# Output projections in 512 columns, weights in units of 1 MB, norm rows kept for the last block, the sample group moved to the third

## The chip, the cores and the metric

The kernel runs on one core of a Trainium2 chip, in one launch. The metric is the time of the launch in device microseconds. The engines are named as in the profile: PE is TensorE (matmuls and transposes), PEld its loads of the stationary operand, DVE is VectorE, ACT is ScalarE, POOL is GpSimd and SP is SyncE, which here only issues transfers (DMAs) in the order of its queue.

## What is computed

One inference step of a decoder trunk of two layers, for a prompt group of 2048 rows and a sample group of 8 rows (one token each, with 2048 cached rows per sequence), which share the weights. The model width is 1024. Cut to what matters here:

```python
for layer in range(2):
    # layer 0: spatial-gating MLP (A) beside stick-breaking attention (B)
    # layer 1: top-256 sparse attention with an indexer (C) beside causal pooling (D)
    hp = mixer(xp @ w_in[layer])          # (2048, 1024)
    hs = mixer(xs @ w_in[layer], cache)   # (8, 1024)
    xp = layer_norm(alpha * xp + hp @ w_out[layer], ln_g[layer], ln_b[layer])
    xs = layer_norm(alpha * xs + hs @ w_out[layer], ln_g[layer], ln_b[layer])
```

All values are float32. The caches' new rows are outputs too.

## The kernel before

**Tiling.** The prompt is cut into four blocks of 512 rows (`TB`). For each block and layer there is an input projection (`p0` for layer 0, `p1a` and `p1b` for layer 1), the mixers (`mixer_b`, and `c_tiles` over 16 query tiles of 128 rows), and an output projection with the norm (`out_proj`, `ln_late`, `ln`). Each projection splits both operands into a high and a low part in the format fp32r and sums three products, high x high, low x high and high x low: L876 to L878 for the input, L1261 to L1263 for the output. The input projection holds 128 columns of weights stationary (`wh`, `wl`) and moves 512 rows of x; the output projection holds 128x128 of the mixers' output (`oh`, `ol`) stationary and moves 256 columns of the weights, into one PSUM tile `pp_o` for each 128 rows. DVE adds `pp_o` to the rows `xres` (L1266).

**Weights.** `plan_w` lists pieces of 512 KB in the order of use, `more_w` loads the next one when a piece has been used, and `load_w` fetches it: raw into `wr`, then ACT copies out the high part (L749) and DVE subtracts to get the low part (L752). Weights of layer 1 are split at the first block and kept in DRAM in two parts; later blocks load both parts (L744). `wh` and `wl` have two buffers each; every third kept piece goes into the two buffers of `wr` instead (`THIRD`).

**Sample group.** Its rows pass through each projection beside one prompt block: `ps_smp` (L894) in the input projection, `ps_so` (L1274) in the output projection. In layer 1 its attention (`sample1`) gathers the cached values through a table of pages with 16 indirect DMAs that POOL issues (L2425, tile `s_vp`, two buffers), and PE uses each gather in L2429 (`ps_sv`). Its last output projection and its norm stand beside the fourth block: `xs_res` are its residual rows, `xpre` its rows before the norm in DRAM, `xs_ln` the rows that are normed.

**Norm.** `ln` computes statistics on DVE (L1325, L1326, a reciprocal root of 15 small operations, then `ln_nb`), scales on ACT (L1339), multiplies with g on POOL (L1340) and adds b on DVE (L1341). The rows of g and b (`lng`, `lnb`) are loaded for each call and half of the columns, 256 KB each (L1335, L1336). The last 128 rows of the last block are projected apart in `out_tail` (L1292 to L1296), when the last attention tile is done; the weights for that lie in a pool `tw`, opened when the pools of the selection (`sel`) close.

**Order of the work.** `run` interleaves streams by estimated costs (`par`), which decides only in which order the program is recorded. Afterwards a planner (`Order`) simulates the engines with its own table of costs and writes a fixed order for each engine and the turn in which tiles get their buffers. Any change of sizes or buffers therefore gives a new order on all five engines. Each engine runs its order strictly in sequence.

Of the kernel before, what the change touches and what calls it, by code (L numbers as in the profile page):

```python
# [11 lines left out]
F32 = mybir.dt.float32  # L12
# [27 lines left out]
THIRD = True  # L40
# [4 lines left out]
KT = 8  # L45
# [654 lines left out]
class Body:  # L700
# [31 lines left out]
    def load_w(self, src, shape, key, pool=None):  # L732
        nc = self.nc
        wr = lambda d, n: self.loc.tile(shape, d, tag="wr", name=n, bufs=self.bufs["wr"])
        new = lambda d, n: (pool or self.wp).tile(shape, d, tag=n, name=n, bufs=4 if pool else 2)
        if shape[2] == 64:
            return self.load_idx(src, key)
# [8 lines left out]
        raw = wr(F32, "wr")  # L746
        nc.sync.dma_start(raw, src)
        hi, lo = new(F32R, "wh"), new(F32R, "wl")
        nc.scalar.copy(hi, raw)  # L749
        h = shape[1] // 2  # L750
        for e, c in ((nc.vector, slice(0, h)), (nc.vector, slice(h, 2 * h))):
            e.tensor_tensor(lo[:, c], raw[:, c], hi[:, c].bitcast(F32), op=OP.subtract)  # L752
        if KEEP.get(key[0]) == key[1]:
            kept = self.kept_w[key[::2]] = [self.dr.tile(shape, F32, name="w%s_%s_%s" % (n, key[0], "_".join(map(str, key[2])) if isinstance(key[2], tuple) else key[2])) for n in "hl"]
            for t, d in zip((hi, lo), kept):
                nc.sync.dma_start(d, t.bitcast(F32))
        return hi, lo

    def load_idx(self, src, key):

        nc = self.nc
        w = self.wp.tile([P, KT, P], F32R, tag="wh", name="wi2")
        kept = self.kept_w.get(key[::2])
        if kept:
            nc.sync.dma_start(w.bitcast(F32), kept)
        else:
            raw = self.loc.tile([P, KT, 64], F32, tag="wr", name="wr", bufs=self.bufs["wr"])
            nc.sync.dma_start(raw, src)
            nc.scalar.copy(w[:, :, 0:64], raw)
            nc.vector.tensor_tensor(w[:, :, 64:P], raw, w[:, :, 0:64].bitcast(F32), op=OP.subtract)  # L770
            kept = self.kept_w[key[::2]] = self.dr.tile([P, KT, P], F32, name="wi2d")
            nc.sync.dma_start(kept, w.bitcast(F32))
        return w[:, :, 0:36], w[:, :, 64:100], w
# [42 lines left out]
    def load_x(self, src):  # L816
# [3 lines left out]
        for kt in range(KT):  # L820
            x = self.otile("xc")
            nc.sync.dma_start(x, src[kt * P:(kt + 1) * P])
# [37 lines left out]
    def proj(self, m, x, smp, c0):  # L860
# [22 lines left out]
        self.more_w()  # L883
# [73 lines left out]
    def plan_w(self, stages):  # L957

        I = self.I
        self.wplan, self.wready, self.kept_w, self.n_kept = [], [], {}, 0  # L960
        for no, st in enumerate(stages):
            key = st, stages[:no].count(st)
            if st[:3] == "out":
                w = I["w_out"][int(st[3])]
                self.wplan += [(w[cg, hf], [P, 4, 256], (*key, (cg, hf)))
                               for cg in range(4) for hf in HALVES[int(st[3])]]
                continue
# [5 lines left out]
            self.wplan += [(w(c, n), [P, KT, 64 if n == 36 else n], (*key, c)) for c, n in cols]  # L973
        for _ in range(2):
            self.more_w()

    def more_w(self, pool=None):
        if self.wplan:
            src, shape, key = self.wplan.pop(0)
            self.wready.append(self.load_w(src, shape, key, pool))  # L980
# [1670 lines left out]
```

## Time and profile before

| what | before |
|---|---|
| median of 3 runs | 2663.24 us (2654.11 to 2670.14) |
| the profiled execution | 2654.22 us |
| its span, first to last instruction | 2652.5 us |
| PE busy | 2552.0 us |
| DVE, ACT, POOL busy | 1951.7, 1483.4, 747.4 us |
| mean granted clock of PE | 0.986 |
| bytes by DMA | 582.34 MB, 220 GB/s over the span |

Busy times are unions over the time axis: matmuls are pipelined, so the sum of their durations is more than PE's busy time, and the distance between two starts says how long one occupies PE. A wait is idle time of an engine, put down to what ended it. "Landing" is when a transfer's data has arrived. The profiled execution is 9.0 us faster than the median of the runs.

### The profile page before, as it was taken

Reading aid. Unit: us, or ns where it says so; the run is one execution under the profiler, and the core shown is the slowest. Engines: PE = TensorE matmul, PEld = TensorE weight load, DVE = VectorE, ACT = ScalarE, POOL = GpSimd, SP = SyncE. Lnnn points to the kernel's source line nnn. Section 1 sums busy time; section 2 is a strip of 40 time slices with the busy share of each in tenths; the row PEclk is TensorE's granted clock in tenths of the full one; section 3 lists DMA queues with packets and bytes.
Section 4 is the critical chain, followed back from the end, with each engine's and each line's share of the span. In section 5 each row is a group of like instructions: output and inputs, shape, how many; then the busy total and the mean of one; then the engine's idle time right before and its main releaser. Section 6 shows DMA issues by size and latency. Waiting matters only on the chain. (4 is left out here: it accounts for less than half of the span.)

```text
span 2652.5 us, 50978 instructions
## 1 busy us (share of the span) xinstructions
PE 2552.0 (96%) x16530; PEld 2032.1 (77%) x16530; DVE 1951.7 (74%) x5338; ACT 1483.4 (56%) x3056; POOL 747.4 (28%) x1024
## 2 busy tenths in 40 slices
PE   8999999999999999998999999999999999999996
PEld 7888787877767787867777777777877788787886
DVE  3576578776957696936877987798797788788745
ACT  3334334444443444434656776786585678788753
POOL 0101113211201313114443633335321243343222
PEclk9999999999999999999999999999899999999998
DMA  8557767786799777745788666543676577667472
GB/s 274 165 174 235 256 195 247 249 275 210 237 317 349 247 247 247 233 139 168 205 281 246 202 189 181 172 142 117 204 245 223 188 246 249 225 231 265 156 261 91
DMA packets 345454, 582.34 MB, mean 220 GB/s; under 512 B 41393, under 2 KB 163411, under 8 KB 345155
## 3 DMA queue, kind: packets, MB, share of 16 engines
q1 hardware_dynamic: 342219, 568.39, 66.9%
q0 software_dynamic: 2944, 10.49, 1.2%
q8 instruction: 131, 2.15, 0.3%
q14 instruction: 160, 1.31, 0.2%
HBM read 460.36 MB, written 118.56 MB: 218 GB/s over the span
## 5 line engine op out<-in xcount | busy, mean ns | idle before, releaser
L876 PE MATMUL pp<-xh,wh 128*128 128x512 f32 x1504 | 613.5, 409 | 4.1 <-DMA wh<-wh_p1a 2.7
L878 PE MATMUL pp<-xh,wl 128*128 128x512 f32 x1504 | 600.7, 400 | 0.3 <-DMA wl<-wl_p1b 0.2
L877 PE MATMUL pp<-xl,wh 128*128 128x512 f32 x1504 | 599.9, 399 | 0.0
L752 DVE TENSOR_TENSOR wl<-wr,wh 128x512 fp32r<-128x512 f32 x342 | 236.4, 712 | 141.4 <-ACT wh L749 116.7
L876 PEld LDWEIGHTS pp<-xh,wh 128*128 128x128 f32 x1504 | 284.0, 189 | 69.7 <-issue 12.2
L878 PEld LDWEIGHTS pp<-xh,wl 128*128 128x128 f32 x1504 | 284.0, 189 | 66.3 <-issue 10.8
L877 PEld LDWEIGHTS pp<-xl,wh 128*128 128x128 f32 x1504 | 284.2, 189 | 55.7 <-issue 7.2
L749 ACT CAST wh<-wr 128x1024 fp32r<-128x1024 f32 x171 | 179.5, 1050 | 257.6 <-PE pp L877 146.3
L1261 PE MATMUL pp_o<-wh,oh 128*128 128x256 f32 x1008 | 293.5, 293 | 14.1 <-ACT oh L724 8.2
L1262 PE MATMUL pp_o<-wl,oh 128*128 128x256 f32 x1008 | 289.4, 288 | 0.0
L1263 PE MATMUL pp_o<-wh,ol 128*128 128x256 f32 x1008 | 287.8, 289 | 0.4 <-POOL ol L730 0.4
L1194 ACT COPY P<-ps_p 128x512 f32<-128x512 f32 (+2 forms) x320 | 165.4, 522 | 195.9 <-PE ps_p L1193 174.2
L1170 DVE TENSOR_TENSOR_SCAN P<-P,bfst 128x512 f32<-128x512 f32 x192 | 250.0, 1318 | 30.1 <-ACT P L1163 23.2
L1899 ACT ACTIVATE zt<-zt,nmax 128x512 f32<-128x512 f32 (+3 forms) x320 | 210.2, 659 | 64.6 <-DVE nmax L1887 64.2
L1914 ACT COPY zt<-ps_pc 128x512 f32<-128x512 f32 (+3 forms) x320 | 164.5, 522 | 101.3 <-PE ps_pc L1912 100.2
L1261 PEld LDWEIGHTS pp_o<-wh,oh 128*128 128x128 f32 x1008 | 193.2, 192 | 26.5 <-ACT oh L724 8.5
L1881 PE MATMUL z_c<-ksc,qc 128*128 128x512 f32 (+3 forms) x640 | 198.8, 393 | 11.7 <-DVE mx L1883 6.1
L1626 ACT ACTIVATE mk<-ix,tk_tn 128x512 int8<-128x512 f32 (+13 forms) x140 | 183.6, 1311 | 35.5 <-DVE tk_tn L1676 28.1
L1883 DVE CUSTOM_DVE_ANT_0 zt<-z_c,mk 128x512 f32<-128x512 f32 (+3 forms) x256 | 147.6, 588 | 69.5 <-PE z_c L1881 39.4
L1263 PEld LDWEIGHTS pp_o<-wh,ol 128*128 128x128 f32 x1008 | 192.2, 192 | 8.3 <-issue 5.5
L1262 PEld LDWEIGHTS pp_o<-wl,oh 128*128 128x128 f32 x1008 | 193.7, 192 | 4.6 <-issue 1.5
L1156 PE MATMUL z<-ks,q 128*128 128x512 f32 (+3 forms) x640 | 190.3, 381 | 4.6 <-DMA ks<-ksc 3.1
(458 smaller groups left out, 5177.4 us busy)
## 6 DMA issues: line engine op xcount, KB each, us to landing
pg<-cache_b_kv SPq DMA_DIRECT2D x256, 256.0 KB
wr<-w_in_even SPq DMA_DIRECT2D x112, 512.0 KB
ks<-ksc SPq DMA_DIRECT2D x80, 256.0 KB
wr<-w_out SPq DMA_DIRECT2D x40, 512.0 KB
ksc<-kcs SPq DMA_DIRECT2D x80, 256.0 KB
wh<-wh_p1b SPq DMA_DIRECT2D x36, 512.0 KB
wl<-wl_p1b SPq DMA_DIRECT2D x36, 512.0 KB
q<-qsc SPq DMA_DIRECT2D x64, 256.0 KB
```

The source lines that it names most:

```text
L752: e.tensor_tensor(lo[:, c], raw[:, c], hi[:, c].bitcast(F32), op=OP.subtract)
L876: nc.tensor.matmul(ps[:m], wh[:, kt, :m], xh[kt], start=a, stop=False)
L877: nc.tensor.matmul(ps[:m], wh[:, kt, :m], xl[kt], start=False, stop=False)
L878: nc.tensor.matmul(ps[:m], wl[:, kt, :m], xh[kt], start=False, stop=b)
L1156: nc.tensor.matmul(z[:, :n], q2[:, c, t * P:(t + 1) * P].bitcast(F32R), ks[:, :n].bitcast(F32R), start=c == 0, stop=c == 1)
L1170: nc.vector.tensor_tensor_scan(r, r, r, initial=ini, op0=OP.mult, op1=OP.bypass)
L1261: nc.tensor.matmul(ps[:, :256], oh[:, tt], wh[:, k], start=a, stop=False)
L1262: nc.tensor.matmul(ps[:, :256], oh[:, tt], wl[:, k], start=False, stop=False)
L1263: nc.tensor.matmul(ps[:, :256], ol[:, tt], wh[:, k], start=False, stop=b)
L1626: nc.scalar.activation(mk.bitcast(I8)[:, :L], x, AF.Sign, bias=t3[:, c:c + 1], scale=-1.0, accum_out=ss[:, c // 2:c // 2 + 1])
L1881: nc.tensor.matmul(z[:, :w], q2[:, c, jj % 2, :].bitcast(F32R), kk, start=c == 0, stop=c == 1)
L1899: nc.scalar.activation(zt, zt, AF.Exp, bias=nmx, accum_out=st["rs"][:, h, c:c + 1])
```

## The change

Output projections now move 512 columns at a time, two groups of columns instead of four, so that one `pp_o` tile fills its PSUM bank. Weights are planned, loaded, kept and released in units of 1 MB of raw weights, that is two pieces of an input projection or half the contraction of 512 columns of an output projection; `wh` and `wl` keep two buffers of this double size. The space comes from the scratch of the dynamic transfers (`dynamic_dma_scratch_size` of 1024 bytes a partition), and `THIRD`, a scratch tile `xwork` and the second buffer of `dwg` go. The first weights are issued after the loads of x begin, with an order among them (`lags`): the second 512 KB after the fourth x tile has landed, the third and fourth after the eighth. The rows of g and b of layer 1 are loaded once, whole, into the pool `tw` for the last block's stage. The sample group goes through the third block's output projection. The norm of the very last 128 rows multiplies with g on DVE and stores each half of the columns apart.

```diff
-    def load_w(self, src, shape, key, pool=None):
+    def load_w(self, parts, key, pool=None):
...
+        U = 2 * KT * P
+        new = lambda n: (pool or self.wp).tile([P, U], F32R, tag=n, name=n, bufs=2)
+        hi, lo = new("wh"), new("wl")
         kept = self.kept_w.get(key[::2])
+        span = slice(KT * P if parts[0][1] == 36 else 0, U)
         if kept:
-            self.n_kept += 1
-            f = wr if THIRD and not pool and self.n_kept % 3 == 0 else new
-            hi, lo = f(F32R, "wh"), f(F32R, "wl")
-            for t, d in zip((hi, lo), kept):
-                nc.sync.dma_start(t.bitcast(F32), d)
-            return hi, lo
...
+            nc.sync.dma_start(hi.bitcast(F32), kept[0])
+            nc.sync.dma_start(lo[:, span].bitcast(F32), kept[1][:, span])
+        out = []
+        for j, (src, n) in enumerate(parts):
...
+            raw = self.loc.tile([P, KT * P], F32, tag="wr", name="wr", bufs=self.bufs["wr"])
+            raw = w3(raw)[:, :, 0:64] if n == 36 else raw
+            d = nc.sync.dma_start(raw, src)
...
+            nc.scalar.copy(todo[0][0], raw)
+            for h, l, q in todo:
+                nc.vector.tensor_tensor(l[:, q], raw[:, q], h[:, q].bitcast(F32), op=OP.subtract)
...
@@ proj
-        self.more_w()
+        if w[-1]:
+            self.more_w()
@@ plan_w
-                self.wplan += [(w[cg, hf], [P, 4, 256], (*key, (cg, hf)))
-                               for cg in range(4) for hf in HALVES[int(st[3])]]
+                self.wplan += [([(w[cg, hf, q], 512) for q in range(2)], (*key, (cg, hf)))
+                               for cg in range(2) for hf in HALVES[int(st[3])]]
...
-        for _ in range(2):
-            self.more_w()
+            for k in range(0, len(cols), 2):
+                unit = cols[k:k + 2]
+                self.wplan.append(([(w(c, n), n) for c, n in unit], (*key, tuple(c for c, _ in unit))))
@@ p0
+        if i == 0:
+            self.more_w()
+            self.more_w()
+            self.lags += [(w.name, self.xdma[k].name) for w, k in zip(self.wdma[1:], (3, 7, 7))]
+            self.wdma = None
@@ out_proj
-        for cg in range(4):
-            ws = {hf: self.wready.pop(0) for hf in HALVES[layer]}
+        for cg in range(2):
+            ws = {hf: self.wready.pop(0)[:2] for hf in HALVES[layer]}
...
-                            nc.tensor.matmul(ps[:, :256], oh[:, tt], wh[:, k], start=a, stop=False)
-                            nc.tensor.matmul(ps[:, :256], oh[:, tt], wl[:, k], start=False, stop=False)
-                            nc.tensor.matmul(ps[:, :256], ol[:, tt], wh[:, k], start=False, stop=b)
+                            nc.tensor.matmul(ps, oh[:, tt], wh[:, k], start=a, stop=False)
+                            nc.tensor.matmul(ps, oh[:, tt], wl[:, k], start=False, stop=False)
+                            nc.tensor.matmul(ps, ol[:, tt], wh[:, k], start=False, stop=b)
                         if hf if some else n:
-                            y = xr[t][:, cg * 256:(cg + 1) * 256]
-                            nc.vector.scalar_tensor_tensor(y, y, ALPHA, ps[:, :256], op0=OP.mult, op1=OP.add)
+                            y = xr[t][:, cg * 512:(cg + 1) * 512]
+                            nc.vector.scalar_tensor_tensor(y, y, ALPHA, ps, op0=OP.mult, op1=OP.add)
...
@@ out_tail
-            y = self.xlast[:, cg * 256:(cg + 1) * 256]
+            y = self.xlast[:, cg * 512:(cg + 1) * 512]
             self.nc.vector.tensor_tensor(y, y, ps, op=OP.add)
-        self.late = self.ln_late([self.xlast], dst[3 * P:TB], None, 1)
-        self.finish()
+        x = self.xlast
+        for _ in self.ln([(x[:, 0:512], x[:, 512:1024])], P, 1, dst[3 * P:TB]):
+            pass
@@ ln
-            g, b = self.tmp("lng"), self.tmp("lnb")
-            nc.sync.dma_start(g, self.bc(self.I["ln_g"][layer, cs], P))
-            nc.sync.dma_start(b, self.bc(self.I["ln_b"][layer, cs], P))
+            if self.gb:
+                g, b = (x[:, cs] for x in self.gb)
+            else:
+                g, b = self.tmp("lng"), self.tmp("lnb")
+                nc.sync.dma_start(g, self.bc(self.I["ln_g"][layer, cs], P))
+                nc.sync.dma_start(b, self.bc(self.I["ln_b"][layer, cs], P))
...
-                nc.gpsimd.tensor_tensor(z, z, g[:n], op=OP.mult)
+                (nc.gpsimd if last is None else nc.vector).tensor_tensor(z, z, g[:n], op=OP.mult)
                 nc.vector.tensor_tensor(z, z, b[:n], op=OP.add)
+                if last is not None:
+                    nc.sync.dma_start(last[:, cs], z)
@@ run
-            self.par([(p1b(3), PC), (o1(0), PO)], [(self.c_tiles(10, 11, 15, False), C(10, 11))], [(take(bg, 26), 26)])
-            self.par([(o1(1), PO), (o1(2), PO)], [(self.c_tiles(12, 14, 15, False), C(12, 14))], [(take(bg, 500), 60)])
+            self.par([(p1b(3), PC), (o1(0), PO)], [(self.c_tiles(10, 11, 15, False), C(10, 11))], [(take(bg, 34), 34)])
+            out = O["y_sample"].rearrange("b t d -> (b t) d")
+            self.par([(o1(1), PO), (o1(2, (self.x1s, out)), PO)], [(self.c_tiles(12, 14, 15, False), C(12, 14))],
+                     [(take(bg, 500), 84)])
...
+            self.gb = [self.tw.tile([P, D], F32, tag=n, name=n, bufs=1) for n in ("lng1", "lnb1")]
+            for x, n in zip(self.gb, ("ln_g", "ln_b")):
+                nc.sync.dma_start(x, self.bc(I[n][1], P))
             self.olast = []
-            self.par([(ended(14), 1), (o1(3, (self.x1s, out), True), PO), (self.late_steps(), 10)],
+            self.par([(ended(14), 1), (o1(3, None, True), PO), (self.late_steps(), 10)],
                      [(self.c_tiles(15, 15, 15, True), C(15, 15))])
@@ kernel
-    nc = bacc.Bacc("TRN2", target_bir_lowering=False, num_devices=1)
+    new = lambda: bacc.Bacc("TRN2", target_bir_lowering=False, num_devices=1, dynamic_dma_scratch_size=1024)
```

Line numbers of the changed kernel differ by some: the output projection's matmuls are L1266 to L1268, the sample's L1279, the norm's multiply and add L1349 and L1350, the gathers L2436 and their use L2440.

**The new order at three places.** PE in the output projection of the first block, where DVE has drained the first two `pp_o` tiles and the next two begin. Before:

```order
L1261 MATMUL pp_o_5346<-wh_5059,oh_5127 128x256
L1262 MATMUL pp_o_5346<-wl_5060,oh_5127 128x256
L1263 MATMUL pp_o_5346<-wh_5059,ol_5128 128x256
L1261 MATMUL pp_o_5346<-wh_5059,oh_5194 128x256
L1262 MATMUL pp_o_5346<-wl_5060,oh_5194 128x256
```

And now:

```order
L1266 MATMUL pp_o_5336<-wh_4912,oh_5080 128x512
L1267 MATMUL pp_o_5336<-wl_4913,oh_5080 128x512
L1268 MATMUL pp_o_5336<-wh_4912,ol_5081 128x512
L1198 MATMUL ps_p_5595<-idf_81,P_5356 128x128 x4
L1207 MATMUL av_5363<-P_5091,vs_5265 64x256
```

The three products of one 128x128 tile of `oh` stand together as before, each over 512 columns, and the same tile of `oh` is loaded half as often.

DVE at the end of the program, from the last statistics to the last add. Before, with rows of the sample group (`xs_ln`) among those of the last rows (128x1):

```order
L1341 TENSOR_TENSOR xres<-xres,lnb 128x512
L786 TENSOR_TENSOR rs_t<-ln_rs 128x1
L787 TENSOR_TENSOR rs_t<-rs_t,rs_a 128x1
L1341 TENSOR_TENSOR xs_ln<-xs_ln,lnb 8x512
L788 TENSOR_SCALAR rs_t<-rs_t 128x1
L1341 TENSOR_TENSOR xs_ln<-xs_ln,lnb 8x512
L789 TENSOR_TENSOR ln_rs<-ln_rs,rs_t 128x1
...
L1330 SCALAR_TENSOR_TENSOR ln_nb<-ln_mv,ln_rs 128x1
L1341 TENSOR_TENSOR xres<-xres,lnb 128x512 x2
```

And now:

```order
L1350 TENSOR_TENSOR xres<-xres,lnb_38447 128x512
L786 TENSOR_TENSOR rs_t<-rs_t,rs_a 128x1
L787 TENSOR_SCALAR rs_t<-rs_t 128x1
L788 TENSOR_TENSOR ln_rs<-ln_rs,rs_t 128x1
...
L1336 SCALAR_TENSOR_TENSOR ln_nb<-ln_mv,ln_rs 128x1
L1349 TENSOR_TENSOR xres<-xres,lng_38446 128x512 x2
L1350 TENSOR_TENSOR xres<-xres,lnb_38447 128x512 x2
```

The sample group's adds are gone from the end, and DVE has taken over the two multiplies with g.

POOL around the second half of the sample group's gathers. Before:

```order
L2425 DMA s_vp<-cache_c_v,s_rq 128x1024 x2
L1340 TENSOR_TENSOR xres<-xres,lng 128x512 x2
L1867 TENSOR_TENSOR nm<-nm,mk 128x256
L2425 DMA s_vp<-cache_c_v,s_rq 128x1024
L1340 TENSOR_TENSOR xres<-xres,lng 128x512
L2425 DMA s_vp<-cache_c_v,s_rq 128x1024
L1340 TENSOR_TENSOR xres<-xres,lng 128x512 x2
L1867 TENSOR_TENSOR nm<-nm,mk 128x256
L2425 DMA s_vp<-cache_c_v,s_rq 128x1024
```

And now:

```order
L2436 DMA s_vp<-cache_c_v,s_rq 128x1024
L1349 TENSOR_TENSOR xres<-xres,lng 128x512
L2436 DMA s_vp<-cache_c_v,s_rq 128x1024
L1349 TENSOR_TENSOR xres<-xres,lng 128x512
L729 TENSOR_TENSOR ol<-ot,oh 128x512
L1349 TENSOR_TENSOR xres<-xres,lng 128x512 x2
L2436 DMA s_vp<-cache_c_v,s_rq 128x1024
L1349 TENSOR_TENSOR xres<-xres,lng 128x512
L2436 DMA s_vp<-cache_c_v,s_rq 128x1024
L1349 TENSOR_TENSOR xres<-xres,lng 128x512 x2
L2436 DMA s_vp<-cache_c_v,s_rq 128x1024 x2
```

The multiplies of a block's norm (`xres`) stand among the gathers in both. From the first to the last use of a gather, PE's order holds 685 rows of matmuls (repeats counted) before, 234 of them `pp_o`, and 396 now, 82 of them `pp_o`.

More of the change, by code (lines that the diff above doesn't have):

```diff
@@ L749, in load_w @@
[L749 to L773, printed above, removed]
+            nc.sync.dma_start(hi.bitcast(F32), kept[0])
@@ new lines, in load_w @@
+            nc.sync.dma_start(lo[:, span].bitcast(F32), kept[1][:, span])
+        out = []
+        for j, (src, n) in enumerate(parts):
+            c = slice(j * KT * P, (j + 1) * KT * P)
+            h, l = hi[:, c], lo[:, c]
+            w3 = lambda x: x.rearrange("p (k n) -> p k n", k=KT)
+            if n == 36:
+                full = w3(h)
+                out.append((full[:, :, 0:36], full[:, :, 64:100], full))
+                todo = [(full[:, :, 0:64], full[:, :, 64:P], slice(0, KT))]
+            else:
+                out.append((w3(h), w3(l)))
+                g = KT * P // 2
+                todo = [(h, l, slice(0, g)), (h, l, slice(g, 2 * g))]
+            if kept:
+                continue
+            raw = self.loc.tile([P, KT * P], F32, tag="wr", name="wr", bufs=self.bufs["wr"])
+            raw = w3(raw)[:, :, 0:64] if n == 36 else raw
+            d = nc.sync.dma_start(raw, src)
+            if self.wdma is not None:
+                self.wdma.append(d.ins)
+            nc.scalar.copy(todo[0][0], raw)
+            for h, l, q in todo:
+                nc.vector.tensor_tensor(l[:, q], raw[:, q], h[:, q].bitcast(F32), op=OP.subtract)
@@ new lines, in load_w @@
+        if not kept and KEEP.get(key[0]) == key[1]:
+            kept = self.kept_w[key[::2]] = [self.dr.tile([P, U], F32, name="w%s_%s_%s" % (n, key[0], "_".join(map(str, key[2])))) for n in "hl"]
+            nc.sync.dma_start(kept[0], hi.bitcast(F32))
+            nc.sync.dma_start(kept[1][:, span], lo[:, span].bitcast(F32))
+        if len(parts) == 2 and parts[0][1] == 512:
+            both = [x.rearrange("p (k n) -> p k n", k=4) for x in (hi, lo)]
+            return [both]
+        return out
@@ L1286, in out_tail @@
     def out_tail(self, ws, dst):
-        for cg, (wh, wl) in enumerate(ws):
-            ps = self.ps("pp_o")[:, :256]
+        for cg, (wh, wl, _) in enumerate(ws):
+            ps = self.ps("pp_o")
             for k in range(4):
@@ L1316, in ln_late, with ln @@
                 nc.sync.dma_start(smp[1][:, c * 512:(c + 1) * 512], xs[c])
-    def ln(self, ys, n, layer):
+    def ln(self, ys, n, layer, last=None):
         nc = self.nc
@@ L1508, in p1b @@
                 base += sh
-            dwg = self.sm.tile([P, P], F32, tag="dwg", name="dwg", bufs=2)
+            dwg = self.sm.tile([P, P], F32, tag="dwg", name="dwg", bufs=1)
             nc.sync.dma_start(dwg, self.I["d_w_grp"][0, g])
@@ L1547, in setup_sel @@
         nc.vector.memset(self.negc, NEG)
-        self.xwork = self.cst.tile([P, 3 * 32], F32, name="xwork")
         self.fq = self.cst.tile([32, 32], F32, name="fq")
@@ L2597, in arrange @@
     parts = lambda w, n: w.reshape(-1, P, w.shape[1] // n, n).transpose(2, 1, 0, 3)
-    a["w_in_even"] = parts(np.asarray(inputs["w_in_even"])[0], P)
+    a["w_in_even"] = parts(np.asarray(inputs["w_in_even"])[0], P).reshape(-1, P, KT * P)
     odd = np.asarray(inputs["w_in_odd"])[0]
-    a["w_in_odd"] = np.stack([parts(odd[:, c:c + P], P)[0] for c in ODD])
+    a["w_in_odd"] = np.stack([parts(odd[:, c:c + P], P)[0].reshape(P, KT * P) for c in ODD])
     a["w_in_idx"] = np.concatenate([parts(odd[:, 896:932], 36)[0], np.zeros((P, KT, 28), np.float32)], axis=2)
-    out = np.asarray(inputs["w_out"]).reshape(2, 2, 4, P, 4, 256)
-    a["w_out"] = out.transpose(0, 4, 1, 3, 2, 5)
+    out = np.asarray(inputs["w_out"]).reshape(2, 2, 2, 2, P, 2, 512)
+    a["w_out"] = out.transpose(0, 5, 1, 2, 4, 3, 6).reshape(2, 2, 2, 2, P, 1024)
     return {n: np.ascontiguousarray(x) for n, x in a.items()}
@@ L2645 @@
     try:
-        build(bacc.Bacc("TRN2", target_bir_lowering=False, num_devices=1), shapes)
+        build(new(), shapes)
     except Planned as x:
```

44 lines of the change are left out of this document (19 added, 25 removed).

## The prediction

> **What bounds the kernel now.** I read the page first: its span, busy times and slices.
>
> ```profile
> span 2652.5 us, 50978 instructions
> PE 2552.0 (96%) x16530; PEld 2032.1 (77%) x16530; DVE 1951.7 (74%) x5338; ACT 1483.4 (56%) x3056; POOL 747.4 (28%) x1024
> ...
> PE   8999999999999999998999999999999999999996
> ...
> PEclk9999999999999999999999999999899999999998
> ```
>
> PE is busy in nine tenths of every slice but the first and the last. PE's 100.5 us without work are 2652.5 - 2552.0. A cut of PE's own work therefore shortens the span wherever it falls, while DVE (74%) and the transfers have room. Next I asked for PE's waits, longest sums first, to see what the 100.5 us consist of.
>
> ```profile
> PE ps_xs L1973 <- DMA x_smp<-x_sample: 9.0, 1, 9.0
> PE pp_o L1261 <- ACT oh L724: 8.2, 2, 7.9
> ...
> PE pp_o L1261 <- DVE xres L1266: 4.7, 6, 3.0
> ...
> PE pp L876 <- DMA wh<-wh_p1a: 2.7, 3, 1.2
> ...
> PE pp_o L1261 <- DMA wh<-wh_out: 0.6, 1, 0.6
> ...
> PE pp L878 <- DMA wl<-wl_p1b: 0.2, 1, 0.2
> ```
>
> Columns: sum, times, longest. Weights that were kept in DRAM cost PE 3.5 us in all (2.7 + 0.6 + 0.2), so a deeper weight buffer has at most that to win from them. The largest single wait is the first, 9.0 us before any matmul. The largest idle stretch is in no list of PE's waits, because nothing follows it: the end, in the timeline.
>
> ```profile
> 2629.38 0.28 PE L1294 MATMUL pp_o<-wh,ll 128*128 128x256 f32 x1
> ...
> 2630.24 0.69 DVE L1325 BATCH_NORM_STATS2 bn<-xres 128x6 f32<-128x512 f32 x1
> ...
> 2639.66 0.68 DVE L1341 TENSOR_TENSOR xs_ln<-xs_ln,lnb 8x512 f32<-8x512 f32 x1 [1.82 <-DMA lnb<-ln_b]
> ...
> 2641.95 0.16 DVE L1330 SCALAR_TENSOR_TENSOR ln_nb<-ln_mv,ln_rs 128x1 f32<-128x1 f32 x1
> 2642.15 1.52 ACT L1339 ACTIVATE xres<-xres,ln_nb,ln_rs 128x512 f32<-128x512 f32 x2 [11.76 <-DVE ln_nb L1330]
> 2644.54 1.26 POOL L1340 TENSOR_TENSOR xres<-xres,lng 128x512 f32<-128x512 f32 x1 [5.58 <-DMA lng<-ln_g]
> 2646.23 1.26 POOL L1340 TENSOR_TENSOR xres<-xres,lng 128x512 f32<-128x512 f32 x1 [0.42 <-DMA lng<-ln_g]
> 2646.76 1.88 DVE L1341 TENSOR_TENSOR xres<-xres,lnb 128x512 f32<-128x512 f32 x2 [4.65 <-DMA lnb<-ln_b]
> 2648.67 0.36 SPq L1308 DMA_DIRECT2D out_y_prompt<-xres  x1
> ```
>
> Columns: start, duration, instruction, and in brackets the idle time before it with what ended it. The last matmul ends at 2629.66, the span at 2652.5: 22.8 us in which PE does nothing. The sample group's norm and the loads of g and b stand in that stretch ahead of the last rows (1.82, 5.58, 4.65 us waited). That leaves 77.7 us of PE idle time inside the program.
>
> **Out projections, the largest term.** How long a matmul occupies PE is the distance from one start to the next, since the durations overlap. The windows give the count, the timeline the first and last start of three unbroken runs.
>
> ```profile
> 446.39:452.16 5.77, 5.76 (x48) 5.71 (x48) 0.41 (x1) 1.00 0.73 249
> 446.40 0.28 PE L1261 MATMUL pp_o<-wh,oh 128*128 128x256 f32 x1
> ...
> 452.03 0.28 PE L1263 MATMUL pp_o<-wh,ol 128*128 128x256 f32 x1
> 26.35:37.12 10.77, 10.76 (x48) 8.90 (x48) 1.36 (x2) 0.87 (x2) 1.00 0.90 274
> 26.36 0.44 PE L876 MATMUL pp<-xh,wh 128*128 128x512 f32 x1
> ...
> 37.11 0.39 PE L878 MATMUL pp<-xh,wl 128*128 128x512 f32 x1
> 813.61:841.10 27.49, 27.48 (x122) 22.72 (x121) 3.39 (x5) 2.44 (x5) 1.00 0.98 372
> 813.62 0.39 PE L876 MATMUL pp<-xh,wh 128*128 128x512 f32 x1
> ...
> 841.05 0.39 PE L877 MATMUL pp<-xl,wh 128*128 128x512 f32 x1
> ```
>
> At 256 columns the step is 5.63/47 = 119.8 ns. At 512 columns, in the input projections, it is 10.75/47 = 228.7 and 27.43/121 = 226.7 ns, with the same operand types and a 128x128 stationary tile. Two matmuls of 256 take 239.6 ns, so one of 512 saves 10.9 to 12.9 ns. There are 3072 of them now (1008 at each of L1261 to L1263, 16 at each of L1292 to L1294) and 1536 then: 16.7 to 19.8 us. I take -18, since the longer run is the steadier, at full clock like the other. The sample matmuls (L1274) go from 128 to 64 by the same rule, under 1 us, and I count nothing. The count of turns from a transpose or an f32 matmul to an fp32r one, which are the places where a step is longer, is 978 in the old order and 982 in the new, so no term comes from there.
>
> A rule of the Trainium skill, TensorE: Matmul & The Clock Gate, section Back-to-back issue gap, speaks for less: it gives an isolated gap of N/2.4 + 2.5 ns, by which 256 columns cost 109 and 512 cost 216, an estimate of 2.5 ns a pair or 4 us in all, and a total saving of 12 instead of 26. The rows disagree: 119.8 where it has 109.
>
> **The end.** What remains after the last matmul, by rows: the add from PSUM now at 512 columns, 0.8 (twice the 256 form); two statistics 1.4 (0.69 each); the small operations, 16 at about 0.19 with their gaps (L1330 at 2641.95 is 0.16), 3.0; five adds of the three earlier row blocks that the new order puts between them, 3.4 (0.68 each); ACT 0.8; two multiplies, now on DVE, and two adds, 2.7; and the last store, 2652.5 - 2648.67 = 3.8 for 512 KB. Sum 15.9, and 22.8 - 15.9 is -7. If the five adds run at the 0.94 of the pair at 2646.76 and the store keeps its length, the gain is 5; if the half-size store takes half of 3.8, it is 9.
>
> **The start.** x_smp and the first x tiles now stand behind one weight of 512 KB, not two.
>
> ```profile
> 4.42 1.04 ACT L749 CAST wh<-wr 128x1024 fp32r<-128x1024 f32 x1 [2.34 <-DMA wr<-w_in_even]
> ...
> 5.69 1.04 ACT L749 CAST wh<-wr 128x1024 fp32r<-128x1024 f32 x1 [0.23 <-DMA wr<-w_in_even]
> ```
>
> The casts start as weights land, 1.27 us apart, so the 9.0 us wait falls by about that; but the second weight is held until the fourth x tile has landed, and PE may meet it later. Between -1.3 and +2 I take -1.
>
> **Weights in pairs.** The same bytes come in transfers of 1 MB, both units hold four columns instead of three, and a unit is released only when its second column is done. Nothing in this trace has that form. Best case: the 3.5 us of waits go. Worst: see the third rival. I take 0, as the waits are near 0.04 us for each of the 85 pieces now. The cover is the other work on PE in those stretches; without it a unit's 2 MB at the 200 GB/s below take 10.5 us.
>
> **Sample group and kept norm rows.** Moving the sample rows into the third block moves 64 matmuls between two stretches in which PE is full: 0. Of its DMAs, the loads of xs_res and the stores to xpre go from four to two each and the two loads and two stores of the norm stay, all now on SP a block earlier; two multiplies of POOL leave the end, counted there. The stores are where SP stands still with other transfers queued behind it:
>
> ```profile
> SPq L1281 <- DVE xs_res L1280: 39.2, 5, 18.0
> ```
>
> In block 3 the weights of the next units stood behind such a wait; in the third block the queue will hold loads of attention and of block 3 instead. Half the stores gives fewer waits, a stall of up to 18 us behind one is the other end; PE's list names no transfer that such a wait delayed by over 3 us, so I take 0. g and b are loaded once instead of per block, behind the release of the last selection's space; the norm of the third block waits for them, and behind it its stores, the loads of xres and the drains of block 3. The trace shows this chain already binding a little:
>
> ```profile
> 2558.60 0.42 DVE L1266 SCALAR_TENSOR_TENSOR xres<-xres,pp_o 128x256 f32<-128x256 f32 x1 [5.04 <-DMA xres<-x]
> ```
>
> That is the 3.0 us wait for xres in PE's list. I count 0 with 3 either way. DVE's drains of 512 columns halve in number, a gain off the path.
>
> **Sum.** -18 - 7 - 1 = -26. The profiled execution took 2654.2 us, so it would take 2628; the median of the three runs is 2663.2, 9 above, and from it the sum gives 2637. I forecast 2633, between them. A new order also redistributes the 77.7 us of inner waits; I let them vary by 12. The forecast's own range is 2612 to 2648.
>
> **Rivals.** *The gathers fall behind.* The sample's 16 gathers have two buffers.
>
> ```profile
> L2429 PE MATMUL ps_sv<-s_vp,s_lg x256: 272/273/278, 2350.0 to 2450.3; 128*8 128x128 f32 x128
> L2425 POOL DMA_INDIRECT s_vp<-cache_c_v,s_rq x16: 937/984/2623, 2319.1 to 2432.9; - x16
> ...
>   PE ps_sv L2429: 15.4, 5
> ...
> DMA to landing us min/median/max: 4.3/6.0/9.2
> ...
> 2377.44 0.62 PE L2429 MATMUL ps_sv<-s_vp,s_lg 128*8 128x128 f32 x16
> ```
>
> Their use on PE spreads over 100 us now, with 685 matmuls from first to last, 234 of them pp_o (28 us by their step). The new order leaves 396, 82 of them pp_o, because the result is wanted a block earlier: 72 us x 314/451 for the others and 19 for pp_o, an estimate of 69 us or 4.6 a gather. A buffer turns over in a landing and a use, 6.0 + 0.6 at the median, so two give one per 3.3 us; at the longest landing and with one norm multiply of 1.26 ahead on POOL, one per 5.5. For: the new order sets such multiplies between gathers, and the margin is gone above a landing of 7.3 us. Against: now POOL waits for PE (15.4 us), not PE for POOL. Price 15 x 0.9 = 14: 2647.
>
> *512 columns cost two times 256.* Then PE's -18 is nothing, and the time is 2652. The page's gap would give most of this. Against it stand two runs of 170 matmuls together.
>
> *A unit arrives late, and it gets slower.* The place is the kept units of the input projections and of layer 1's output.
>
> ```profile
> 1200.00:2200.00 1000.00, 965.63 (x6365) 762.36 (x6366) 810.82 (x2741) 671.10 (x1481) 368.56 (x523) 0.98 0.65 200
> ```
>
> Columns: PE, PEld, DVE, ACT and POOL busy, clock, DMA share, GB/s. About 30 kept units lie there and 14 after; 10.5 us for 2 MB stand against 10.9 us (48 x 227) that the other unit lasts when PE does nothing else. Each microsecond a unit is late costs 44 us: 2677 with one. It cancels the gain at 0.6 us a unit and makes the kernel slower by 0.5% from 0.9. For: the margin in a dense run is 0.4 us, and the third buffer is gone. Against: a unit has 33 us of the stretch on average (1000/30), and 0.04 us a piece is what the waits are.
>
> **How the numbers follow.** Forecast 0.70; gathers 0.14; no PE saving 0.07; late units 0.09. About 0.5%, 13 us, is what a measurement here can tell from no change, so faster means under 2650. Faster: nearly all of the first (0.66), half of the second (0.07), under half of the third (0.03): 0.76. Slower: 0.08 of the last. Same: the rest, 0.16. The range 2608 to 2660 takes in the first three cases, and leaves out the late units and the tails.
>
> **What would show it.** In the profile after: pp_o steps of 227 to 229 ns; PE busy near 2530; about 16 us from the last matmul to the end, with no wait for lng or lnb there; PE's waits for wh and wl still under 5 us in all; no wait of PE at the ps_sv matmuls. I am wrong if PE's inner idle time rises above 95 us, or if the 512-column step is above 235.

## The result, and the profile after

The changed kernel takes 2694.68 us (median of 5 runs, 2690.74 to 2696.62) against 2662.91 us (5 runs, 2654.11 to 2670.14): ratio 1.0122, 95% interval 1.0103 to 1.014. It is slower by 1.2%, where 2633 us and a range of 2608 to 2660 were forecast. The profiled execution took 2690.74 us with a span of 2689.0, 36.5 more than the span before.

The page of the changed kernel, its span, busy times and the rows of PE and its clock:

```profile
span 2689.0 us, 47275 instructions
PE 2555.0 (95%) x14930; PEld 1945.0 (72%) x14930; DVE 1960.9 (73%) x5266; ACT 1490.7 (55%) x3056; POOL 748.9 (28%) x1022
...
PE   8999999999999999999899999999799999979997
...
PEclk9999999999999999999999999999799999979999
```

The 1600 matmuls fewer are there (x14930 for x16530), but PE's busy time is 3 us longer, not 18 shorter, and three slices besides the ends show less than nine tenths, where the page before has one. In the view of spans and clocks the granted clock fell; first line before, second after:

```profile
core 0: 2652.5 us, clock 0.986
core 0: 2689.0 us, clock 0.975
```

The unbroken run of output projections below (timeline, its first and last start) gives the new step: 21.36/94 = 227.2 ns, as the input projections had it.

```profile
1843.00 0.39 PE L1267 MATMUL pp_o<-wl,oh 128*128 128x512 f32 x1
...
1864.36 0.39 PE L1268 MATMUL pp_o<-wh,ol 128*128 128x512 f32 x1
```

The end, in the timeline: the last matmul starts at 2671.85 and the span closes at 2689.0; from the last matmul's end it is 16.8 us. The multiplies of the last rows are on DVE, and no wait for g or b stands there.

```profile
2671.85 0.39 PE L1299 MATMUL pp_o<-wh,ll 128*128 128x512 f32 x1
...
2681.99 1.52 ACT L1348 ACTIVATE xres<-xres,ln_nb,ln_rs 128x512 f32<-128x512 f32 x2 [8.82 <-DVE ln_nb L1336]
2682.83 1.40 DVE L1349 TENSOR_TENSOR xres<-xres,lng 128x512 f32<-128x512 f32 x2 [0.88 <-ACT xres L1348]
...
2684.86 0.94 SPq L1352 DMA_DIRECT2D out_y_prompt<-xres  x2
```

PE's waits of the changed kernel (sum, times, longest), longest sums first:

```profile
PE z_c L1892 <- DVE mx L1894: 13.5, 10, 4.0
PE ps_pc L1923 <- ACT zt L1925: 8.1, 5, 4.9
PE ps_xs L1984 <- DMA x_smp<-x_sample: 7.0, 1, 7.0
PE ps_p L1198 <- ACT P L1199: 6.7, 3, 5.5
...
PE ps_sm L2177 <- DVE s_s L2245: 5.8, 1, 5.8
PE pp_o L1266 <- DMA wh<-wh_out: 4.3, 2, 2.6
...
PE ps_sv L2440 <- DMA s_vp<-cache_c_v,s_rq: 0.9, 1, 0.9
```

The same three waits in the kernel before:

```profile
PE z_c L1881 <- DVE mx L1883: 6.1, 7, 2.6
...
PE ps_pc L1912 <- ACT zt L1914: 2.8, 4, 1.6
...
PE ps_p L1193 <- ACT P L1194: 1.2, 1, 1.2
```

Waits that were 6.1 (attention scores held up by DVE), 2.8 and 1.2 us (transposes held up by ACT's copies) are now 13.5, 8.1 and 6.7, and some are new, as that of the sample's `ps_sm`. PE's idle time inside the program is 117.3 us where it was 77.7.

The idle time is not the whole price. In the clock's records PE ran at half speed for 54.6 us before the last matmul, and now for 122.9. PE was busy in 45.1 and 94.1 us of these, and half of that is counted as lost, 22.5 and 47.0 us. (In such a record of the changed kernel, from 1868.8 to 1871.4 us, a step of 512 columns takes 427 ns instead of 227, so a little less than half is lost.) The 36.5 us of span are then idle time +39.6, half clock +24.5, tail -6.0, and PE's work at full clock -21.5 (2529.4 to 2507.9; the parts are rounded). Nothing can be left over in this sum, since the work is what remains of PE's busy time.

### The profile page after: what moved, and what is told of

The parts are those of the page before. It is cut to its first block, busy times and chain, and to the rows that moved or that the text cites. A ratio compares the mean times of both kernels' runs of the same rounds, so it can differ in the third digit from the quotient of the medians.

```text
span 2689.0 us, 47275 instructions
## 1 busy us (share of the span) xinstructions
PE 2555.0 (95%) x14930; PEld 1945.0 (72%) x14930; DVE 1960.9 (73%) x5266; ACT 1490.7 (55%) x3056; POOL 748.9 (28%) x1022
## 5 line engine op out<-in xcount | busy, mean ns | idle before, releaser
L764 DVE TENSOR_TENSOR wl<-wr,wh 128x512 fp32r<-128x512 f32 x342 | 229.0, 701 | 82.2 <-ACT wh L762 70.3
L1636 ACT ACTIVATE mk<-ix,tk_tn 128x384 int8<-128x384 f32 (+13 forms) x140 | 183.3, 1310 | 79.8 <-DVE tk_tn L1686 39.0
L1892 PE MATMUL z_c<-ksc,qc 128*128 128x512 f32 (+3 forms) x640 | 198.9, 398 | 21.5 <-DVE mx L1894 13.5
L1266 PE MATMUL pp_o<-wh,oh 128*128 128x512 f32 x504 | 206.4, 413 | 8.0 <-DMA wh<-wh_out 4.3
L1268 PE MATMUL pp_o<-wh,ol 128*128 128x512 f32 x504 | 203.6, 409 | 4.2 <-POOL ol L729 4.2
L1267 PE MATMUL pp_o<-wl,oh 128*128 128x512 f32 x504 | 204.8, 408 | 0.0
L1878 POOL TENSOR_TENSOR nm<-nm,mk 128x256 f32<-128x256 f32 (+1 forms) x128 | 96.8, 757 | 369.9 <-DMA nm<-bft 167.6
L1923 PE MATMUL ps_pc<-idf,zt 128*128 128x128 f32 x1088 | 179.2, 279 | 13.6 <-ACT zt L1925 8.1
L1198 PE MATMUL ps_p<-idf,P 128*128 128x128 f32 x1088 | 183.5, 276 | 9.0 <-ACT P L1199 6.7
```

The costliest lines, as they stand in the source:

```text
L764: nc.vector.tensor_tensor(l[:, q], raw[:, q], h[:, q].bitcast(F32), op=OP.subtract)
L1266: nc.tensor.matmul(ps, oh[:, tt], wh[:, k], start=a, stop=False)
L1267: nc.tensor.matmul(ps, oh[:, tt], wl[:, k], start=False, stop=False)
L1268: nc.tensor.matmul(ps, ol[:, tt], wh[:, k], start=False, stop=b)
L1892: nc.tensor.matmul(z[:, :w], q2[:, c, jj % 2, :].bitcast(F32R), kk, start=c == 0, stop=c == 1)
L1923: nc.tensor.transpose(pt[:, k, :], zs[c][:, k * P:(k + 1) * P], self.idf)
```

## The experiments

"PE work" below is PE's busy time less half of what it was busy at half clock. "Orders" are what the kernel's planner writes; the same program has several, by the guesses and seeds it starts from. Times are medians, beside runs of the kernel before on the same chip (2660 to 2664 us).

**Undoing one part.** Sample group back in the fourth block:

```
- self.par([(p1b(3), PC), (o1(0), PO)], ..., [(take(bg, 34), 34)])
- self.par([(o1(1), PO), (o1(2, (self.x1s, out)), PO)], ..., [(take(bg, 500), 84)])
+ self.par([(p1b(3), PC), (o1(0), PO)], ..., [(take(bg, 26), 26)])
+ self.par([(o1(1), PO), (o1(2), PO)], ..., [(take(bg, 500), 60)])
- (o1(3, None, True), PO)
+ (o1(3, (self.x1s, out), True), PO)
```

> The changed kernel, with the sample group's output rows put back into the fourth block of layer 1 (and the shares of the sample work in the second and third block back to 26 and 60); all else of the change stays. Theory S (the sample group, wanted a block earlier, squeezes the sample's attention into a stretch where PE then waits): PE's inner idle time falls from 117 to under 90 us, the time at half clock before the last matmul from 123 to under 85 us, and the time to 2635 to 2655. Theory C (512 columns hold the two PSUM banks of the output projections twice as long, and PE runs out of other work): little changes, 2680 to 2700. Theory P (every change redraws the order of all engines, and one order is some tens of us better than another without any one part being to blame): anywhere between 2640 and 2700, with idle time spread in new places.

2657.77 us, ratio 0.9979 (0.9962 to 0.9995): 37 less than the changed kernel. Idle 95.0 us (S: under 90), half clock 78.5 (S: under 85), the time 3 us over S's range. That is nearest to S, but only one of its three marks is met, and P allows it too.

256 columns again, the two halves of a unit one after the other:

```
+ q = slice(cg % 2 * 256, cg % 2 * 256 + 256)
- nc.tensor.matmul(ps, oh[:, tt], wh[:, k], start=a, stop=False)
+ nc.tensor.matmul(ps[:, :256], oh[:, tt], wh[:, k, q], start=a, stop=False)
```

> The changed kernel, with the output projections of the prompt issued at 256 columns again, two halves of the unit one after the other; units, sample group and kept norm rows stay. The PE work lost is 18 us by the prediction's steps. Theory S: about 2694 + 18 = 2712, inner idle time still over 105 us. Theory C: idle time back under 90 us and the time at or under 2680. Theory P: 2660 to 2740, not to be told from the part undone.

2664.55 us, ratio 1.0009 (0.9993 to 1.0025), idle 86.7. PE's work rose to 2533.0, so 25 us of work came back and yet the time fell by 30: C's reading, and against S. Two different undoings each repair the kernel, which is what P says.

The same instructions in another order:

```
- GUESSES = ((1.0, 200), (1.0, 250), (1.04, 230))
+ GUESSES = ((1.0, 210), (1.0, 240), (1.02, 230))
- draws = [self.draw(k) for k in range(self.DRAWS)]
+ draws = [self.draw(k + 2) for k in range(self.DRAWS)]
```

> The changed kernel, with nothing changed but three guesses and the two seeds by which its planner chooses among orders: the same instructions in another order. Theories S and C: within 13 us of 2694, with PE idle in the same places (around 1880 and 2390 us). Theory P: more than 13 us away, either side, with the idle time elsewhere.

2647.11 us, ratio 0.9944 (0.9922 to 0.9965): 48 us less with no instruction changed. Idle 85.1, half clock 47.8. One of the places that made the difference (16.2 us idle against 3.6), in windows of the changed kernel and then of this one (columns as in the prediction: PE, PEld, DVE, ACT and POOL busy, clock, DMA share, GB/s):

```profile
1860.00:1880.00 20.00, 16.69 (x66) 13.22 (x66) 10.48 (x29) 0.00 (x0) 0.17 (x1) 0.91 0.38 114
1880.00:1900.00 20.00, 7.07 (x26) 4.68 (x24) 14.80 (x79) 5.53 (x17) 4.24 (x9) 0.64 0.90 300
```

```profile
1860.00:1880.00 20.00, 18.48 (x84) 13.67 (x83) 18.23 (x89) 6.87 (x24) 4.26 (x9) 0.91 0.84 256
1880.00:1900.00 20.00, 17.95 (x147) 12.95 (x145) 17.07 (x73) 18.09 (x48) 9.97 (x11) 1.00 0.97 291
```

The timeline of the changed kernel names the wait:

```profile
1876.39 0.37 SPq L1806 DMA_DIRECT2D mkd<-mk  x1
...
1883.62 1.04 ACT L2158 ACTIVATE s_sg<-hT 128x8 f32<-128x8 f32 x8 [24.26 <-DMA mkd<-mk]
...
1886.68 1.56 PE L2177 MATMUL ps_sm<-s_pl,s_dwg 128*128 128x8 f32 x6 [5.80 <-DVE s_s L2245]
1888.43 0.60 PE L2177 MATMUL ps_sm<-s_pl,s_dwg 128*128 128x8 f32 x2 [0.20 <-DVE s_pl L2174]
1892.45 0.22 PE L1998 MATMUL ps_tok<-idf,hT 36*8 36x36 f32 x1 [3.42 <-DVE rs_t L785]
```

Here the space of one stage is handed to the next, once the second selection mask is stored. The store went out at 1876.39 (1857.9 in the other order), ACT stood 24 us, PE ran out of output projections at 1880.9, and what came first afterwards was the sample's chain of short steps, at half clock.

g and b loaded for each norm again:

```
- self.gb = [self.tw.tile([P, D], F32, tag=n, name=n, bufs=1) for n in ("lng1", "lnb1")]
- for x, n in zip(self.gb, ("ln_g", "ln_b")):
-     nc.sync.dma_start(x, self.bc(I[n][1], P))
```

> The changed kernel, with g and b loaded for each norm again, as before, rather than kept behind the last selection; the shorter tail's norm on DVE stays. Theory G (the norm of the third block waits for g and b, and behind it the xres tiles of the last block): 2665 to 2680 and no wait of PE on xres. Theories S and C: 2690 to 2700, the tail 1 to 4 us longer since the last loads come late. Theory P: 2660 to 2730.

2684.62 us, ratio 1.0073 (1.0046 to 1.0101), idle 113.7, tail 17.0. The time lies between the ranges of G and of S and C, and PE still waits 2.9 us for `xres`, so G's two marks are missed; no theory gains. The 10 us are less than the orders of one program differ by, so the kept rows aren't shown to cost anything.

**Do orders scatter for the kernel before too?** The same exchange of guesses and seeds, and the order that the planner ranked second:

```
- if best is None or x < best[0]:
-     best = x, self.order, self.after, self.slot
+ best.append((x, len(best), self.order, self.after, self.slot))
+ ... = sorted(best, key=lambda b: b[:2])[1]
```

> The kernel before, with the same three guesses and two seeds exchanged as in the run that gave the changed kernel another order (2647 against 2695). Theory P (the orders that the planner makes of one program differ by tens of us on the chip, for both kernels alike): 2640 to 2690, most likely 5 to 25 us away from 2664 on either side. Theory U (the kernel before is robust, its orders agree, and only the changed kernel's orders scatter): 2657 to 2671.

> The kernel before, with its own guesses and seeds, but with the order that its planner ranked second of the fifteen it tried. Theory P: 2640 to 2690, away from 2664 by 5 us or more. Theory U: 2657 to 2671. If the planner's ranking means something on the chip, it is 2664 or slower.

2663.65 (1.0013; 0.9996 to 1.003) and 2666.04 us (1.0022; 1.0001 to 1.0043). P was wrong for this kernel: its three orders agree, U. For the changed kernel, second and third pick ([1] and [2]):

> The changed kernel, with its own guesses and seeds, but with the order that its planner ranked second of fifteen. Theory P: 2640 to 2695, likelier under the 2695 of the first than over it, since that one had 117 us of inner idle time against 78 to 114 in all others run so far. If the change itself were slower whatever the order: 2685 or more, which the 2647 of the other order already speaks against.

> As the last, with the order ranked third. Theory P: 2640 to 2700, and the time of each run is its PE work at full clock (2508 to 2521 us), plus its inner idle time, plus half of the busy time at half clock, plus 16 to 18 us of tail: within 3 us of the span.

2680.95 (1.0076; 1.0051 to 1.0101) and 2679.74 us (1.0072; 1.0047 to 1.0097). PE work, idle time, half of the half clock and tail add up to the span by construction; the check is that the work is steady, 2513.3 and 2519.6. So far 2647 is the exception among four orders of the changed kernel.

**Both parts in further orders.** The edits are those above, joined; the third set of guesses is (1.0, 220), (1.02, 200), (1.02, 250).

> The changed kernel with the sample group back in the fourth block (2658 in the order its own guesses gave) and with the three guesses and two seeds exchanged. Theory S (the squeezed sample group is what makes most orders of the changed kernel slow): the other order is good too, 2635 to 2660, inner idle time under 95 us. Theory P (any order of any 512-column kernel is a draw between 2645 and 2695): 2645 to 2695, most likely near 2675.

> The changed kernel with 256 columns in the output projections (2665 in its own order), guesses and seeds exchanged. Theory C (the long steps of 512 columns make orders bad and scattered): again 2655 to 2672. Theory S: the one good order was luck, 2680 to 2715. Theory P: 2650 to 2710.

> The changed kernel with both undone, 256 columns and the sample group in the fourth block: units of 1 MB, kept norm rows, the start and the shorter tail are left of the change. By the sum (tail -6, start -1, no PE saving) 2655 to 2660; if units of 1 MB, four columns in two buffers without the third, are what makes PE wait (theory W), 2670 or more with inner idle time over 95 us.

> The changed kernel as it is, with a third set of guesses and seeds. Its orders so far: 2695, 2681, 2680 from one set of guesses, 2647 from another. Theory S or C (this program's orders are mostly bad, 2647 was luck): 2670 to 2700. Theory O (only the first set of guesses is bad for it): 2640 to 2660.

2638.08 us with the sample group in the fourth block (0.9911; 0.9894 to 0.9927), idle 83.0: S. 2703.46 with 256 columns (1.0161; 1.0142 to 1.018): theory C falls, 256 columns don't repair it, and 2664.55 was one order's luck. 2671.37 with both undone (1.0042; 1.0022 to 1.0063), 11 us over what the sum gave: the time that W (here the units of 1 MB) gave, but with idle 86.7 us without its mark. In this one order units of 1 MB aren't shown to cost anything, nor is the tail's gain visible. 2681.42 for the changed kernel with the third set (1.0068; 1.0045 to 1.009): S or C, not O.

**The sample's move by itself.** It was made alone on the kernel before, and undone again in a third order; and the third block's weights, which the sample matmuls share, were taken out of it by a pass of its own:

```
- if smp and tp[0] == 0:
+ if smp and layer == 0 and tp[0] == 0:
- (o1(2, (self.x1s, out)), PO)]
+ (o1(2, (self.x1s, out)), PO), (self.sample_out((self.x1s, out), 1), 4)]
- "out1", "out1", "out1", "out1", "out1"])
+ "out1", "out1", "out1", "out1", "out1", "out1"])
```

> The changed kernel, in which the sample group of layer 1 no longer shares the third block's weights: it comes right behind that block with four units of its own, which are loaded a second time (8 MB more of loads). Its result is still wanted a block earlier than before. Theory H (in the third block the sample matmuls sit between the two halves of the prompt's, so the first half's units are held from about 2370 us until the sample's attention is done at about 2477; no output weight is loaded for over 100 us, and PE lacks the second half's 44 us of work in that stretch): third-block loads no longer pause for 100 us, PE idle between 2300 and 2500 us falls from 23 to under 14 us, and the time is 2640 to 2662. Theory E (what costs is that the sample's attention itself is pressed, held weights or not): idle there stays over 20 us and the time at 2670 to 2695. Theory P (orders alone): 2645 to 2695, with the pause gone all the same.

> As the last, with the second set of guesses and seeds, so that the two orders can be told from chance. Theory H: 2630 to 2660. Theory E: 2670 to 2700. Theory P: anywhere in 2640 to 2695.

> The kernel before, with one part of the change alone: the sample group's rows in the third block of layer 1 (and the shares 34 and 84 of the sample work); 256 columns, units of one column, old tail stay. Theory H: the first quarter's units are held until the sample's attention is done, three quarters of the block (66 us of PE work) come after it: 2675 to 2700, PE idle between 2300 and 2500 us over 18 us where it was 8. Theory P or a cost that only 512 columns bring: 2657 to 2672.

> The changed kernel with the sample group in the fourth block, third set of guesses and seeds (its orders so far: 2658 and 2638; the changed kernel with that third set: 2681). Theory H: 2635 to 2662, PE idle between 2300 and 2500 us under 15 us. Theory P: as likely over 2665 as under.

The own pass took 2689.55 (1.0092; 1.0063 to 1.012) and 2674.59 us (1.0049; 1.0032 to 1.0066), 5 us less and 27 more than the changed kernel with these sets: H falls. E's times come true, and P allows them too. The pause was real; in the changed kernel's timeline of the queue no output weight is issued for 114 us:

```profile
2369.12 0.40 SPq L740 DMA_DIRECT2D wh<-wh_out  x1
2483.41 0.32 SPq L740 DMA_DIRECT2D wh<-wh_out  x1
```

With the own pass it is 74 and 81 us, and idle time between 2300 and 2500 us is 13.9 and 20.7 us, against 23.0 and 24.4 of the changed kernel with these sets (E had it over 20); but to 2600 it is 27.4 and 36.5, against 30.1 and 27.9. The next 100 us lost what these had won; there PE starts no output projection of the prompt for 61 and 59 us. The pause alone doesn't make a kernel slow either: the order that took 2647 us has one of 124. The move alone on the kernel before: 2663.19 (1.001; 0.9994 to 1.0025), nothing. The sample group in the fourth block in the third set: 2634.97 (0.9898; 0.9878 to 0.9918), the fastest here and faster than both kernels.

**Taking the wait for the attention away.** The sample's output group multiplies rows that are ready early, and the attention's result is left out of the sample's output:

```
- sx = self.sample_split()
+ sx = self.sample_split(self.early if layer else self.os_)
+ self.early = s1["hT"][:, 8:16, :]
```

> The changed kernel, in which the sample's output group of layer 1, still in the third block, multiplies the sample rows of the layer's input projections (ready from the start of the stage) in place of the attention's result; all of the sample's attention is still computed, and what is wrong is only the rows of the sample's output. So the group, and the units it holds, no longer wait for the attention. Theory W (waiting of the out projections' weights, and of all that comes behind them, for the sample's attention is what costs): no pause of 100 us in the loads of output weights, PE idle between 2300 and 2600 us falls from 30 to under 20 us, and the time from 2695 to 2635 to 2665. Theory P (orders alone) or a cost of the other parts: 2670 to 2700, with idle there still over 25 us.

> The same with the third set of guesses and seeds, with which the changed kernel took 2681 (PE idle between 2300 and 2600 us 45 us) and the one with the sample group in the fourth block 2635 (12 us). Theory W: 2630 to 2660 and under 20 us idle there. Theory P: 2660 to 2695.

2669.35 (1.0021; 1.0002 to 1.0039) and 2670.4 us (1.0025; 1.0008 to 1.0043): 25 and 11 us better than the changed kernel in these sets, but short of W (here the wait for the attention); idle in 2300 to 2600 is 26.0 and 32.0 us, and the pauses in the weights are 107 and 123 us. The group's rows were ready early, and still the fixed order put it at 2459 and 2461 us, little ahead of the 2477 and 2468 of the changed kernel in these sets; in the first of the two:

```profile
1838.88 0.22 DVE L729 TENSOR_TENSOR osx<-hT,osx 128x64 fp32r<-128x64 f32 x1
...
2458.82 0.42 PE L1279 MATMUL ps_so<-wh,osx 128*40 128x512 f32 x1
```

So the units were held about as long as before, and these two kernels don't tell what an early group would give.

**What all of them show together.** With 512 columns, the five orders of the changed kernel take 2695, 2681, 2680, 2647 and 2681 us, mean 2677; the three with the sample group in the fourth block 2658, 2638 and 2635, mean 2644. Set by set the difference is 37, 9 and 46 us, and 2647 lies within the other three's range, so the 33 us between the means are rough. On average 30 of them lie between 2300 and 2600 us: idle time and half-clock loss there are 47.3, 55.2, 42.7, 37.5 and 65.7 us against 31.4, 13.7 and 15.4. (In the changed kernel's own order this stretch holds 29 of the 64 us that idle time and half clock rose by; the place near 1880 us is among the others.) The windows from 2300 to 2500, of before, of the changed kernel with the third set, and with the sample group in the fourth block and that same set:

```profile
2300.00:2400.00 100.00, 95.77 (x930) 78.86 (x929) 86.94 (x292) 81.98 (x176) 46.47 (x47) 1.00 0.68 218
2400.00:2500.00 100.00, 96.39 (x898) 84.80 (x895) 80.54 (x281) 81.11 (x166) 32.38 (x41) 1.00 0.62 211
```

```profile
2300.00:2400.00 100.00, 81.37 (x566) 60.11 (x562) 81.06 (x244) 69.61 (x137) 40.77 (x42) 0.89 0.60 194
2400.00:2500.00 100.00, 80.59 (x608) 58.85 (x609) 57.36 (x191) 52.10 (x116) 19.87 (x29) 0.86 0.50 164
```

```profile
2300.00:2400.00 100.00, 95.51 (x759) 68.62 (x757) 87.67 (x277) 80.49 (x168) 43.79 (x47) 0.98 0.68 223
2400.00:2500.00 100.00, 94.28 (x756) 74.76 (x756) 75.32 (x275) 80.08 (x167) 32.33 (x42) 0.97 0.54 177
```

PE's waits there, for the last two in the same order:

```profile
PE ps_sv L2440 <- DMA s_vp<-cache_c_v,s_rq: 14.0, 6, 4.3
PE z_c L1892 <- DVE mx L1894: 13.0, 6, 4.2
PE ps_pc L1923 <- ACT zt L1910: 5.8, 4, 4.8
PE ps_so L2446 <- ACT s_tmp L2444: 2.9, 3, 2.2
```

```profile
PE z_c L1892 <- DVE mx L1894: 6.9, 4, 5.5
PE pp_o L1266 <- DVE xres L1271: 1.4, 1, 1.4
```

In every kernel with 512 columns and the early sample (the own pass and the group that doesn't wait among them) PE waits 7.7 to 19.8 us between 2300 and 2600 us at or for an instruction of the sample's attention; in every other kernel 0 to 3.8. Output projections are the work that could cover such waits, and they run dry: the windows of `pp_o` alone, for the last two in the same order (PE, PEld, DVE busy, clock, DMA share, GB/s):

```profile
2420.00:2440.00 20.00, 0.00 (x0) 0.00 (x0) 0.00 (x0) 0.74 0.47 145
2440.00:2460.00 20.00, 0.00 (x0) 0.00 (x0) 0.00 (x0) 0.91 0.36 100
```

```profile
2420.00:2440.00 20.00, 6.14 (x20) 3.46 (x20) 0.67 (x1) 0.94 0.78 269
2440.00:2460.00 20.00, 7.34 (x21) 3.72 (x21) 0.00 (x0) 0.89 0.19 54
```

The longest time between two starts of `pp_o` there is 18.6 to 60.7 us in the ten kernels with 512 columns and the early sample, and 12.3 to 14.5 in the three with the sample in the fourth block. That fits PE meeting steps that nothing is left to cover, but it doesn't prove it: the order that took 2647 us has 36.6, and with 256 columns 39.0 went with 2665 us and 29.2 with 2703.

Shown, then: the same instructions differ by 48 us with their order; the sample group's earlier place costs some 33 us on average in the 512-column kernel, nearly all between 2300 and 2600 us, and nothing measurable in one order of the kernel before. Not settled: through what. A pass of its own, at 8 MB more of loads, didn't repair it, which speaks against the sharing of the third block's weights; whether the group's holding of them does it is open. The shares 34 and 84 of the sample's work, which place its attention among the other work in the program that the planner starts from, went with the move in all these kernels and were not changed alone; nor is it settled why 256 columns gave 2665 in one order and 2703 in another, where the waits at the sample are under 2 us.

## Why the prediction was wrong, step by step

- **Out projections, -18:** right. PE's work at full clock is 2532.0 us on average over the seven kernels with 256 columns (2528.9 to 2535.3) and 2514.2 over the thirteen with 512 (2507.9 to 2520.8): -18. The rival that 512 columns cost two times 256 is out. By the gap that the Trainium skill gives (TensorE: Matmul & The Clock Gate, Back-to-back issue gap) 4 us, an estimate, would have been saved; the trace disagrees, with 119.8 and 227.2 ns.
- **The end, -7:** -6.0, 16.8 us where 15.9 was worked out. **The start, -1:** -2.0 (the wait for the sample's x went from 9.0 to 7.0).
- **Weights in pairs, 0:** PE's waits for them are 5.3 us (4.3, 0.8 and 0.2), 1.8 more; the rival of the late units didn't come.
- **Sample group and kept rows, 0 with 3 either way: this is the step that failed.** It took the move for 64 matmuls between two stretches in which PE is full, and weighed the group's matmuls and transfers. It did not price what the earlier due date does to the order of the rest: 33 us on average. PE isn't full there any more; from 2300 to 2500 us it was busy for 192.2 us before and 177.0 now. Through which wait this comes stays open.
- **The inner waits, varying by 12:** they rose by 39.6. The spread was not worked out from anything; the changed kernel's own orders have 85 to 117 us. The one that was run takes 18 us more than their mean, which is the luck of the draw.
- **Nothing was put down for the clock,** though the quoted page showed an inner slice of PEclk under nine (and one of PE, which the prediction read over) and the third rival's row a clock of 0.98. Idle time is paid again behind each wait: 24.5 us on top of 39.6.
- **The gathers falling behind** were a rival at 14 us. In the profile after, the uses spread over 85.5 us where 69 were estimated, and PE waited 0.9 us there; in the third set 14.0. That the sum agrees there is luck: it was priced as 15 waits of 0.9 us, and came as 6 of up to 4.3.
- **The signs:** idle over 95 us was to mean that the forecast is wrong, and it was 117. Of those named for the profile after, the step and the end came as said; PE busy is 2555 and not near 2530, the waits for `wh` and `wl` are just over 5 us, and PE did wait a little at `ps_sv` (0.9 and 0.6).

With the sample group left in the fourth block the times, 2635 to 2658, lie in the forecast's range of 2608 to 2660, all above 2633. So the miss of 62 us is 33 for the sample's move, 18 for the order that was drawn, and 11 that stay in the mean without the move and were not traced.

## What to carry to other kernels

Where a planner or scheduler places the work, a change has two prices: its own instructions, which rows give to a few us, and the new order, which they don't. Judge it over several orders of both kernels before believing either sign. Price an edit that makes a long chain due earlier by the other work that covers the chain's waits, and count idle time of a saturated PE with the half clock behind it.

## What the runs showed of the hardware

Waits of 1.5 to 3 us already cost clock. Over the twenty profiles, half clock begins within some 3 us of a PE gap of 1 to 1.5 us in 22% of 218 cases, of 1.5 to 2 us in 51% of 87, of 2 to 3 us in 66% of 132, and of 3.5 us or more in 89% of 85; of gaps under 1 us 10% have one near. Part of this is a neighbour's doing. Among gaps that stand alone, with no other of 0.1 us or more within 7 us, half clock follows within 3 us after none of 62 of 1 to 1.5 us, 19 of 35 of 1.5 to 2 us, 28 of 44 of 2 to 3 us, and all 62 of 3 us or more; so in these profiles clock is lost from some 1.5 us on. Half clock comes in pieces of 3.4 us or a multiple of that. The Trainium skill, TensorE: Matmul & The Clock Gate, section Part 1: The HAM clock gate, has the array throttled to half after an idle window of about 3.4 us; the length of the pieces agrees, but here gaps of half that length were followed by half clock in every second case.
